# Decays between tokens from two matmuls with fixed weights instead of four float32 ones

## The chip, the cores and the metric

The kernel runs on one core of a Trainium2 chip. The metric is the device time of one execution in microseconds (us), as the median of several runs.

## The reference

Two layers of a decoder trunk on 256 tokens of width 1024. Each layer is SwiGLU, layer norm, three token mixers side by side (a gated delta rule, a sliding-window attention and a cross attention to a memory), their gated sum, layer norm, SwiGLU, layer norm. The change lies in the delta rule. There every token has a log decay g for each of four heads, and the weight with which token i acts on a later token c of the same block is the exponent of the sum of g over the tokens after i up to c:

```
g = jnp.cumsum(g, axis=-1)
tril = jnp.tril(jnp.ones((C, C), bool))
decay = jnp.exp(jnp.where(tril, g[..., :, None] - g[..., None, :], NEG_INF))
a = jnp.where(strict, jnp.einsum('bhncd,bhnsd->bhncs', k_beta, k) * decay, 0.0)
qk = jnp.where(tril, jnp.einsum('bhncd,bhnsd->bhncs', q, k) * decay, 0.0)
```

The kernel computes the same with blocks of 128 tokens in place of 64.

## The kernel before

Tokens come in two blocks of 128 (index c or tb). Weights stream from HBM in one fixed order, as units of 128x1024 float32. A unit is split on the chip: ACT casts it to fp32r (whi), DVE subtracts that from the original (wlo, L123), and every large product is three fp32r matmuls, high by high, high by low, low by high (mm3). Five buffers each for whi and wlo rotate, and the split of a unit begins when PE gives a buffer back.

The two FFN stages of a layer enclose the mixers. In the mixers PE's order is fixed by the program: the projections are generators that yield after each unit, and weave puts small steps of the mixers between the units. The other engines' orders come from a planner that goes by the order of the program and by when it expects operands; they are fixed before the run, and each engine takes its instructions in that order.

The steps around the change, in PE's order:

- the projection of the memory queries, four units with two tiles each (256 columns), with tok_v after the third;
- one unit for the keys and values of the window;
- the projection of the window queries, four units. After the first, decay (sums of g from the start of a block, 8 columns). After the second, spread(0) and x_scores(0), the latter twelve matmuls of 256 columns. After the third, spread(1). After the fourth, products(0, 0) and products(0, 1);
- the gates' units, with 512 columns, and in them x_scores(1), products(1, ...) and the inverses, which GpSimd (POOL) computes for blocks of 16.

g itself comes from a chain of some twenty small DVE operations on 128x8 (L607 to L631). GpSimd makes the product of a triangle with g for both blocks (L671, into TM[c][:, 0]). spread(c) turns that product, as the weights, into a bank of PSUM with four matmuls of 128 columns, one per head, against the other triangle (tri). DVE adds the mask dtm (L656) and ACT takes the exponent (L657). products(c, hh) multiplies keys by keys and keys by queries and DVE scales the result by the decays (L668).

Of the kernel before, what the change touches and what calls it, by code (L numbers as in the profile page):

```python
# [11 lines left out]
F32R = mybir.dt.float32r  # L12
I32 = mybir.dt.int32
AF = mybir.ActivationFunctionType
ALU = mybir.AluOpType
AX = mybir.AxisListType

P = 128
# [20 lines left out]
def tile_trunk(ctx, tc, x, xT, mem, memT_, wst, lnp, memln, cvw, rows, cst, out):  # L39
    nc = tc.nc  # L40
# [3 lines left out]
    pc = ctx.enter_context(tc.tile_pool(name="pc", bufs=1))  # L44
    praw = ctx.enter_context(tc.tile_pool(name="praw", bufs=4))
    pu = ctx.enter_context(tc.tile_pool(name="pu", bufs=1))
    p2 = ctx.enter_context(tc.tile_pool(name="p2", bufs=2))
# [7 lines left out]
    def nm(s):  # L55
        uid[0] += 1
        return f"{s}_{uid[0]}"
# [4 lines left out]
    def T(pool, shape, tag, dt=F32, bufs=None):  # L62
        pool = pn if pool is pu and tag in NEAR else pool
        kw = {} if bufs is None else {"bufs": bufs}
        return pool.tile(shape, dt, tag=tag, name=nm(tag), **kw)
# [7 lines left out]
    def sm():  # L73
        return T(psS, [P, 512], "sm")
# [7 lines left out]
    tri = cs[:, C_TRI:C_TRI + P]  # L82
    mlt = cs[:, C_LT:C_LT + P]
    dtm = cs[:, C_DTM:C_DTM + P]

    def over4(ap):
        return ap.unsqueeze(1).to_broadcast([P, 4, ap.shape[-1]])
# [34 lines left out]
    def split(hi, lo, src):  # L122
        return nc.scalar.copy(hi, src).ins, nc.vector.tensor_tensor(lo, src, hi.bitcast(F32), op=ALU.subtract).ins  # L123
# [3 lines left out]
    def pe(ins):  # L127

        return tc.keep_in_program_order(ins) if pinned[0] else ins

    def matmul(*a, **k):
        return pe(nc.tensor.matmul(*a, **k))  # L132
# [10 lines left out]
    def weave(work, steps):  # L143

        for n, _ in enumerate(work, 1):
            for f in steps.get(n, ()):
                f()

    def projB(xt, nt, kpu, behind=None):
        g = projB_parts(xt, nt, kpu, behind)  # L150
        while True:
            try:
                next(g)
            except StopIteration as e:
                return e.value

    def projB_parts(xt, nt, kpu, behind=None):
        banks = [acc().rearrange("p (t s) -> p t s", t=2) for _ in range((nt + 1) // 2)]
        for uu in range(KD // kpu):
            hi, lo = unit(behind=behind)  # L160
            for kk in range(kpu):
                k = uu * kpu + kk
                for t in range(nt):
                    c = (kk * nt + t) * P
                    o = banks[t // 2][:, t % 2, :]
                    lastt = t % 2 == 1 or t == nt - 1
                    matmul(o, hi[:, c:c + P], xt[0](k), start=(k == 0 and t % 2 == 0), stop=False, skip_group_check=True)
                    matmul(o, hi[:, c:c + P], xt[1](k), start=False, stop=False, skip_group_check=True)
                    matmul(o, lo[:, c:c + P], xt[0](k), start=False, stop=(k == KD - 1 and lastt), skip_group_check=True)
            yield  # L170
        return banks

    def halves(xt, use):

        for i in range(2):
            (b,) = yield from projB_parts(xt, 2, 4)
            use(i, b)
# [66 lines left out]
    def acc_of(t):  # L244
        return (lambda k: t[0][:, k, :], lambda k: t[1][:, k, :])
# [183 lines left out]
    def begin(nxt, hT):  # L429
        nxt.first(hT, 0)  # L430
        nxt.first(hT, 1)
        nxt.out(0, nxt.bank)
# [72 lines left out]
    def memory_kv(mT, behind):  # L505
        mx = (lambda k: mT[k // 4][:, k % 4, :], lambda k: mT[2 + k // 4][:, k % 4, :])
        mkT = (T(pu, [P, 4, S], "u10", F32R), T(pu, [P, 4, S], "u7", F32R))
        for i, b in enumerate(projB(mx, 4, 2)):
            split(*(t[:, 2 * i:2 * i + 2, :] for t in mkT), b)
        mv_ = T(pu, [P, 2, 512], "u11")  # L510
        outs = [[acc()] for _ in range(2)]
        projA(mx, 512, 2, KD, outs, behind=behind, held=range(4))
        for tb in range(2):
            nc.scalar.copy(mv_[:, tb, :], outs[tb][0])
        return mkT, mv_

    def mixers(l, hT, mkT, mv_, post):
        xt = acc_of(hT)
# [79 lines left out]
        def col(tag):  # L598
            return T(pu, sh, tag)
# [30 lines left out]
        g = col("g")  # L630
# [15 lines left out]
        TM = [T(pu, [P, 2, 4, P], f"w{2 + c}") for c in range(2)]  # L646
        AK = [T(pu, [P, 4, 2, P], f"u{12 + c}") for c in range(2)]
        hb = lambda ap: ap.unsqueeze(2).to_broadcast([P, 4, P])

        def spread(c):  # L650

            gm, dt = TM[c][:, 0], TM[c][:, 1]
            ps = sm().rearrange("p (h c) -> p h c", h=4)
            for h in range(4):
                matmul(ps[:, h, :], gm[:, h, :], tri, start=True, stop=True)
            nc.vector.tensor_tensor(dt, ps, over4(dtm), op=ALU.add)  # L656
            nc.scalar.activation(dt, dt, AF.Exp)  # L657

        def products(c, hh):
# [6 lines left out]
            for j in range(2):  # L666
                h = 2 * hh + j
                nc.vector.scalar_tensor_tensor(AK[c][:, h], TM[c][:, 1][:, h, :].unsqueeze(1).to_broadcast([P, 2, P]), cS[:, c, h:h + 1], ps[:, j], op0=ALU.mult, op1=ALU.mult)  # L668

        for c in range(2):  # L670
            nc.gpsimd.tensor_tensor(TM[c][:, 0], over4(mlt), hb(g[:, c, :]), op=ALU.mult)  # L671


        xq = (T(pu, [P, 4, S], "u4", F32R), T(pu, [P, 4, S], "u6", F32R))
# [139 lines left out]
        def use_sq(i, b):  # L814
            split(*(t[:, 2 * i:2 * i + 2, :] for t in sq_), b)

        weave(halves(xt, use_xq), {3: [tok_v]})
        (b,) = projB(xt, 1, 8)
        for kv in range(2):
            hs = slice(kv * 64, kv * 64 + 64)  # L820
            split(swk[0][hs, kv, :], swk[1][hs, kv, :], b[hs, 0, :])
        weave(halves(xt, use_sq), {
            1: [decay],
            2: [lambda: spread(0), lambda: x_scores(0)],
            3: [lambda: spread(1)],
            4: [lambda: products(0, 0), lambda: products(0, 1)]})

# [243 lines left out]
    ps = sm()  # L1071
# [7 lines left out]
    def xres(tb):  # L1079
        load(hres[tb], x[tb * P:(tb + 1) * P, :])  # L1080

    def small():
        load(rw, rows.rearrange("l r -> (l r)").partition_broadcast(P))
        load(cw, cvw)

    ends = None
    for l in range(NL):
        mT = []
        mid = memory_T(mT, l)
        if l == 0:  # L1090

            more = {4: lambda *a: xres(0), 6: lambda *a: xres(1), 8: lambda *a: small()}
        post = Post(lnp[l, 0, 0], lnp[l, 0, 1])
        f1.rest(hT, 4, [((pu, "u0"), (pu, "u1")), ((pu, "u2"), (pu, "u3"))], post, mid, ends, {} if l else more)
        kv = memory_kv(mT, post.end)
        if l == 0:
            nc.scalar.activation(nea, rw[:, :, 8:12], AF.Exp)
            nc.vector.tensor_scalar(nea, nea, -1.0, None, ALU.mult)
        post2 = Post(lnp[l, 1, 0], lnp[l, 1, 1])
        mixers(l, post.hT, *kv, post2)  # L1100
        f2 = Ffn()
        begin(f2, post2.hT)
        last = l == NL - 1
        post = Post(lnp[l, 2, 0], lnp[l, 2, 1], last)
        f2.rest(post2.hT, 6, [((pu, a), (pu, b)) for a, b in (("u0", "u1"), ("u2", "u3"), ("u4", "u5"), ("u6", "u13"))], post, behind=post2.end)
        ends = post.end
        if not last:
            f1, hT = Ffn(), post.hT
            begin(f1, hT)
# [87 lines left out]
```

## Time and profile before

| what | before |
|---|---|
| median of 3 runs | 1274.8 us (1274.46 to 1275.08) |
| the profiled execution's own time | 1274.36 us |
| its span, first to last instruction | 1272.6 us |
| PE, PE weight loads | 1260.9 us (99%), 1073.9 us (84%) |
| DVE, ACT, GpSimd | 865.0 us (68%), 660.8 us (52%), 206.9 us (16%) |
| DMA | 261.40 MB, mean 205 GB/s |

Busy times of PE are of overlapping matmuls, whose ends are modelled; what a matmul costs in a stream is read from the distance of the starts.

### The profile page before, as it was taken

Reading aid. Unit: us, or ns where it says so; the run is one execution under the profiler, and the core shown is the slowest. Engines: PE = TensorE matmul, PEld = TensorE weight load, DVE = VectorE, ACT = ScalarE, POOL = GpSimd, SP = SyncE. Lnnn points to the kernel's source line nnn. Section 1 sums busy time; section 2 is a strip of 40 time slices with the busy share of each in tenths; the row PEclk is TensorE's granted clock in tenths of the full one; section 3 lists DMA queues with packets and bytes.
Section 4 is the critical chain, followed back from the end, with each engine's and each line's share of the span. In section 5 each row is a group of like instructions: output and inputs, shape, how many; then the busy total and the mean of one; then the engine's idle time right before and its main releaser. Section 6 shows DMA issues by size and latency. Waiting matters only on the chain.

```text
span 1272.6 us, 18763 instructions
## 1 busy us (share of the span) xinstructions
PE 1260.9 (99%) x6948; PEld 1073.9 (84%) x6948; DVE 865.0 (68%) x1271; ACT 660.8 (52%) x980; POOL 206.9 (16%) x365
## 2 busy tenths in 40 slices
PE   9999999999999999999999999999999999999997
PEld 6888889999878888888888888899987788888886
DVE  5788576897657776665676665759867388666555
ACT  6556444655664544544454554456556564444541
POOL 0232100002311102221012220000024101122200
PEclk9999999999999999999999999999999999999999
DMA  8988755655534748777667877556453356577772
GB/s 296 305 274 280 254 209 164 206 166 142 171 118 138 245 135 264 240 242 221 218 208 242 255 254 215 182 184 213 152 168 133 100 185 229 172 247 244 241 231 73
DMA packets 77499, 261.40 MB, mean 205 GB/s; under 512 B 11904, under 2 KB 13056, under 8 KB 77408
## 3 DMA queue, kind: packets, MB, share of 16 engines
q1 hardware_dynamic: 66320, 232.53, 56.1%
q0 software_dynamic: 11088, 27.68, 7.8%
q8 instruction: 54, 0.88, 0.3%
q14 instruction: 37, 0.30, 0.1%
HBM read 246.40 MB, written 13.76 MB: 204 GB/s over the span
## 4 chain that ended last, share of the span: by engine, by line
PE 96%; DVE 2%; DMA 1%; ACT 1%; issue 0%; SPq 0%; DVEq 0%; ACTq 0%
PE acc L132 85%; PE at L132 4%; PE sm L132 3%; PE sm L135 2%; DVE wlo L123 1%; DMA raw<-in_wst_dram 1%; PE acc L326 1%; PE acc L327 1%; PE acc L329 1%; PE at L135 1%; ACT whi L123 1%; DVE h L289 0%; DVE pp L734 0%; DVE w L938 0%; SPq L115 0%
## 5 line engine op out<-in xcount | busy, mean ns | idle before, releaser
L123 DVE TENSOR_TENSOR wlo<-raw,whi 128x1024 fp32r<-128x1024 f32 (+2 forms) x403 | 488.8, 1220 | 284.9 <-ACT whi L123 282.8
L123 ACT CAST whi<-raw 128x1024 fp32r<-128x1024 f32 (+2 forms) x403 | 413.5, 1033 | 403.7 <-PE acc L132 322.0
L132 PE MATMUL acc<-whi,hT 128*128 128x512 f32 (+1 forms) x1824 | 562.7, 386 | 0.9 <-ACT whi L123 0.9
L132 PEld LDWEIGHTS acc<-whi,hT 128*128 128x128 f32 x1824 | 340.3, 188 | 70.1 <-ACT whi L123 2.5
L132 PE MATMUL acc<-wlo,hT 128*128 128x512 f32 (+1 forms) x912 | 350.3, 384 | 0.5 <-DVE wlo L123 0.5
L132 PE MATMUL acc<-whi,u 128*128 128x512 f32 x812 | 259.6, 392 | 0.0
L132 PEld LDWEIGHTS acc<-wlo,hT 128*128 128x128 f32 x912 | 171.4, 188 | 33.5 <-DVE wlo L123 1.2
L132 PEld LDWEIGHTS acc<-whi,u 128*128 128x128 f32 x812 | 152.3, 188 | 32.1 <-DVE u L123 0.5
L132 PE MATMUL acc<-wlo,u 128*128 128x512 f32 x406 | 158.2, 390 | 0.0
L356 POOL DMA_DIRECT2D tr<-t x176 | 96.3, 554 | 304.5 <-DVE t L350 296.4
L132 PE MATMUL acc<-hT,whi 128*128 128x256 f32 x672 | 122.2, 284 | 0.0
L132 PEld LDWEIGHTS acc<-hT,whi 128*128 128x128 f32 x672 | 104.6, 192 | 0.0
L132 PE MATMUL acc<-hT,wlo 128*128 128x256 f32 x336 | 95.0, 283 | 0.0
L132 PEld LDWEIGHTS acc<-wlo,u 128*128 128x128 f32 x406 | 76.3, 188 | 15.3
L132 PEld LDWEIGHTS acc<-hT,wlo 128*128 128x128 f32 x336 | 64.3, 192 | 0.0
L357 POOL DMA_DIRECT2D pt<-tr x44 | 25.0, 569 | 200.1 <-DMA tr<-t 129.1
L347 ACT ACTIVATE t<-acc 128x256 f32<-128x256 f32 x88 | 33.5, 380 | 37.1 <-PE acc L132 37.1
L132 PE MATMUL acc<-u,u 128*128 128x512 f32 x186 | 46.4, 394 | 0.0
L348 DVE TENSOR_TENSOR t<-t,acc 128x256 f32<-128x256 f32 x88 | 36.6, 416 | 8.6 <-ACT t L347 5.3
L993 POOL TENSOR_TENSOR u<-u,gt 128x512 f32<-128x512 f32 x16 | 20.7, 1295 | 124.9 <-DVE gt L991 124.9
L132 PEld LDWEIGHTS acc<-u,u 128*128 128x128 f32 x186 | 34.6, 188 | 7.5
L546 DVE SCALAR_TENSOR_TENSOR t<-acc,cw,t 128x255 f32<-128x255 f32 (+2 forms) x72 | 34.4, 478 | 1.0
(236 smaller groups left out, 1158.3 us busy)
## 6 DMA issues: line engine op xcount, KB each, us to landing
raw<-in_wst_dram SPq DMA_DIRECT2D x409, 512.0 KB, 4.4
tr<-t POOLq DMA_DIRECT2D x176, 64.0 KB, 3.9
pt<-tr POOLq DMA_DIRECT2D x44, 256.0 KB, 4.9
raw<-in_wst_dram SPq DMA_DIRECT2D x16, 324.0 KB, 3.0
gB<-in_lnp_dram SPq DMA_DIRECT2D x6, 512.0 KB, 5.4
bB<-in_lnp_dram SPq DMA_DIRECT2D x6, 512.0 KB, 6.2
w<-dr POOLq DMA_DIRECT2D x4, 512.0 KB, 11.0
t<-in_xT_dram SPq DMA_DIRECT2D x4, 256.0 KB, 5.4
```

The source lines that it names most:

```text
L123: return nc.scalar.copy(hi, src).ins, nc.vector.tensor_tensor(lo, src, hi.bitcast(F32), op=ALU.subtract).ins
L132: return pe(nc.tensor.matmul(*a, **k))
L135: return pe(nc.tensor.transpose(*a))
L326: nc.tensor.matmul(ps, hT[0][:, k, ts], hi[:, c], start=k == 0, stop=False)
L327: nc.tensor.matmul(ps, hT[0][:, k, ts], lo[:, c], start=False, stop=False)
L329: nc.tensor.matmul(ps, hT[1][:, k, ts], hi[:, c], start=False, stop=k == KD - 1)
L347: act = nc.scalar.activation(t[:, :, tb, :], g, AF.Silu).ins
L348: ins = nc.vector.tensor_tensor(t[:, :, tb, :], t[:, :, tb, :], u, op=ALU.mult).ins
L356: nc.gpsimd.dma_start(d[:, :, q].rearrange("b c x -> c b x"), z[32 * q:32 * q + 32].rearrange("c (b x) -> c b x", b=4))
L357: back = nc.gpsimd.dma_start(y, d.rearrange("b c q x -> (b c) (q x)")).ins
L546: nc.vector.scalar_tensor_tensor(yc[:, j, d:], b[:, j, :S - d], w[:, t:t + 1], yc[:, j, d:], op0=ALU.mult, op1=ALU.add)
L993: nc.gpsimd.tensor_tensor(mg[tb][:, js], mg[tb][:, js], gt[tb][:, js], op=ALU.add)
```

## The change

The triangle that was a weight's mask and the triangle that was streamed change places. GpSimd now multiplies tri by g. The new step spread_parts(c) splits that product into a high and a low fp32r part, in a tile of the pool p2 under the tag of the gates' tiles; the steps are placed after the first and the third unit of the memory queries. spread(c) then issues two matmuls of 512 columns, all four heads at once, with the fixed triangle `later` as weights for both: the high part and the low part, summed in the bank. `later` is an fp32r copy of mlt, made once by ACT, in the first layer.

```
+    later = pc.tile([P, P], F32R, name="later")
...
         def spread(c):
 
-            gm, dt = TM[c][:, 0], TM[c][:, 1]
+            dt = TM[c][:, 1]
             ps = sm().rearrange("p (h c) -> p h c", h=4)
-            for h in range(4):
-                matmul(ps[:, h, :], gm[:, h, :], tri, start=True, stop=True)
+
+            for n in range(2):
+                matmul(ps, later, gms[c][n], start=n == 0, stop=n == 1)
             nc.vector.tensor_tensor(dt, ps, over4(dtm), op=ALU.add)
             nc.scalar.activation(dt, dt, AF.Exp)
...
+        gms = {}
         for c in range(2):
-            nc.gpsimd.tensor_tensor(TM[c][:, 0], over4(mlt), hb(g[:, c, :]), op=ALU.mult)
+            nc.gpsimd.tensor_tensor(TM[c][:, 0], over4(tri), hb(g[:, c, :]), op=ALU.mult)
+
+        def spread_parts(c):
+            both = T(p2, [P, 2, 4, P], "gt", F32R)
+            gms[c] = both[:, 0], both[:, 1]
+            split(*gms[c], TM[c][:, 0])
...
-        weave(halves(xt, use_xq), {3: [tok_v]})
+        weave(halves(xt, use_xq), {1: [lambda: spread_parts(0)], 3: [tok_v, lambda: spread_parts(1)]})
...
         if l == 0:
+            nc.scalar.copy(later, mlt)
```

## Rows read from the trace of the kernel before

**Rows 1.** The page's engine summary: busy time, share of the span, instructions.

```profile
span 1272.6 us, 18763 instructions
PE 1260.9 (99%) x6948; PEld 1073.9 (84%) x6948; DVE 865.0 (68%) x1271; ACT 660.8 (52%) x980; POOL 206.9 (16%) x365
```

**Rows 2.** Waits of PE, whole span: total us, times, longest; first and last of five.

```profile
PE sm L1073 <- DVE pp L1070: 1.5, 1, 1.5
...
PE sm L132 <- DVE w L938: 0.3, 2, 0.2
```

**Rows 3.** Chain of waits, the spreads of both layers: start us, us, what.

```profile
284.73 0.89 PE sm L132 x8
...
289.92 0.89 PE sm L132 x8
...
914.24 0.89 PE sm L132 x8
...
919.43 0.89 PE sm L132 x8
```

**Rows 4.** View of the tile sm, spread's matmuls: duration ns min/median/max, first and last start.

```profile
L132 PE MATMUL sm<-cs,w x32: 270/275/275, 284.6 to 920.0; 128*128 128x128 f32 x32
```

**Rows 5.** Timeline of PE, first layer: start us, us, operation, count.

```profile
284.57 1.05 PE L132 MATMUL sm<-cs,w 128*128 128x128 f32 x8
285.38 1.66 PE L132 MATMUL at<-u,u 128*128 128x256 f32 x12
286.88 0.40 PE L132 MATMUL acc<-hT,whi 128*128 128x256 f32 x2
...
289.76 1.05 PE L132 MATMUL sm<-cs,w 128*128 128x128 f32 x8
...
293.53 0.39 PE L132 MATMUL sm<-u 128*128 128x128 f32 x2
```

**Rows 6.** Timeline of PE, second layer, the first units of the gates.

```profile
925.28 0.63 PE L132 MATMUL acc<-whi,hT 128*128 128x512 f32 x2
925.75 0.39 PE L132 MATMUL acc<-wlo,hT 128*128 128x512 f32 x1
925.97 0.63 PE L132 MATMUL acc<-whi,hT 128*128 128x512 f32 x2
...
927.59 1.57 PE L132 MATMUL at<-u,u 128*128 128x256 f32 x12
929.00 0.38 PE L132 MATMUL sm<-u 128*128 128x128 f32 x2
```

**Rows 7.** View of the tile u: splits of 128x512 read from SBUF.

```profile
L123 ACT CAST u<-pt x44: 611/612/622, 41.8 to 1221.7; 128x512 fp32r<-128x512 f32 x44
L123 DVE TENSOR_TENSOR u<-pt,u x44: 646/650/693, 43.9 to 1223.0; 128x512 fp32r<-128x512 f32 x44
```

**Rows 8.** Timeline of POOL, first layer; in brackets idle time before and its releaser.

```profile
279.52 3.02 POOL L671 TENSOR_TENSOR w<-cs,g 128x512 f32<-128x512 f32 x2 [48.68 <-DVE g L631]
```

**Rows 9.** Timeline of DVE, first layer.

```profile
279.27 0.17 DVE L631 TENSOR_TENSOR g<-spp,nea 128x8 f32<-128x8 f32 x1
279.53 2.11 DVE L123 TENSOR_TENSOR wlo<-raw,whi 128x1024 fp32r<-128x1024 f32 x1
...
283.48 1.23 DVE L123 TENSOR_TENSOR wlo<-raw,whi 128x1024 fp32r<-128x1024 f32 x1 [0.64 <-ACT whi L123]
...
284.81 0.69 DVE L644 TENSOR_TENSOR u<-u,ks 128x512 f32<-128x512 f32 x1
285.66 0.69 DVE L656 TENSOR_TENSOR w<-sm,cs 128x512 f32<-128x512 f32 x1 [0.16 <-PE sm L132]
```

**Rows 10.** Timeline of ACT, first layer.

```profile
278.45 1.05 ACT L123 CAST whi<-raw 128x1024 fp32r<-128x1024 f32 x1 [1.35 <-PE acc L132]
...
282.01 0.37 ACT L123 CAST swk<-acc 64x256 fp32r<-64x256 f32 x1 [2.25 <-DVE swk L123]
...
283.47 0.18 ACT L640 ACTIVATE eg<-sm 128x16 f32<-128x16 f32 x1
```

## Prediction, made before the changed kernel was built

> **What bounds the kernel now.** I read the views from coarse to fine. The engine summary comes first: TensorE (PE) is busy for 1260.9 of the 1272.6 us between the first and the last instruction, VectorE (DVE) for 68% and ScalarE (ACT) for 52% [rows 1]. Next the list of waits for PE: five groups stand in it, from 1.5 us down to 0.3 us, and with the three between them (0.9, 0.5, 0.4) they come to 3.6 us over the whole kernel [rows 2]. PE waits for almost nothing, so time taken from its stream should be time taken from the kernel, and work added to DVE or ACT is free until it makes PE wait. The chain of waits says the same for the place of the change: in it the eight records of one call of spread stand as a piece of PE work of their own, 0.89 us long, twice in each layer and so four times in all [rows 3]. No wait stands between these pieces and their neighbours.
>
> **The removed matmuls.** Each spread issues four float32 matmuls of 128 columns. The trace has each of them as two records: 32 records for 2 layers, 2 token blocks and 4 heads [rows 4]. From the start of the first record at 284.57 to that of the next matmul at 285.38 is 0.81 us, so 0.10 us a record [rows 5]. The durations of 270 to 275 ns say nothing of this, since records overlap; starts are what to compare. There is a second, smaller part. The twelve score matmuls that follow this spread take 1.50 us from their first start to the start of what follows (285.38 to 286.88) [rows 5]; the same twelve in the next stage, which follow fp32r matmuls, take 1.41 us (927.59 to 929.00) [rows 6]. So going from float32 back to fp32r costs about 0.08 us, and that goes too. Together a spread costs 0.89 us, the figure of the chain.
>
> **The added matmuls.** Two fp32r matmuls of 512 columns, with `later` as weights, once with the high and once with the low part of the masked decays. The gate stage has matmuls of exactly that kind (128x128 weights, 512 columns, fp32r): three of them run from 925.28 to 925.97, 0.23 us each [rows 6]. Two are 0.46 us. As bounds for the pair I take 0.45 us (the score matmuls of 256 columns run at 1.41 / 12 = 0.118 us, so 256 more columns cost 0.113, and 1024 columns without any fixed part four times that) and 0.54 us (0.46 and one more change of 0.08 us, if going from 256 to 512 columns costs what the change of type does). The value 0.46 is from rows of the same operation, so I take it.
>
> The PE sum: 0.89 - 0.46 = 0.43 us for a spread, four spreads, 1.7 us; with the bounds 1.4 to 1.8 us.
>
> **The added splits.** spread_parts puts one ACT copy and one DVE subtraction of 128x512 from SBUF on those engines for each block. The same pair with SBUF input is in the trace as the split of the turned FFN tiles: 612 ns on ACT, 650 ns on DVE [rows 7]. Four of each add 2.4 us to ACT and 2.6 us to DVE over the kernel. The question is whether the first low part is there when PE comes to it, as PE's order is fixed in this stage and a late operand stops all that is behind it. The path in the first layer (the second repeats it 629.5 us later, by the pieces of the chain [rows 3]): g is done at 279.44 [rows 9]; the two GpSimd products run from 279.52 to 282.54, 1.51 us each, so that of block 0 ends at 281.03 [rows 8]. ACT then has nothing to do until 282.01 [rows 10], so the copy may end at 281.64. DVE comes free of its weight split at 281.64, and is idle for 0.64 us of the time before 283.48 [rows 9]. That weight split took 2.11 us where its neighbour at 283.48 took 1.23 us, and it ran beside the GpSimd products. With the same stretch, 650 ns becomes 1.1 us, and the low part is ready near 282.8. PE wants the high part at 284.57 and the low part 0.23 us later, at 284.80. The margin is 2.0 us. For block 1 the inputs come 1.5 us later and PE wants them 5.2 us later, so that one has more.
>
> The Trainium skill bears on that stretch: "SBUF — State Buffer", section "Who interferes with whom", says that the only contention is for the port pair that DVE shares with GpSimd, and that it is an exclusive lock, held for a whole instruction. By it the low part of block 0 could not begin before the second product ends at 282.54, and would end at 283.2: a margin of 1.6 us in place of 2.0. The row of 2.11 us agrees only in part, as a subtraction that had waited out the first product to 281.03 could not have been done before 282.2 and was done at 281.64. Either way the sum stays, and only the stall below comes a little nearer.
>
> What is queued behind the added work: on ACT and DVE these are the weight splits. ACT's cast at 278.45 began when PE gave up a buffer [rows 10]; five buffers rotate, so what is cast there is used some four units later, and a unit is 2.9 us of PE work (286.88 to 289.76) [rows 5]. A delay of a microsecond or two is covered by that; without cover each late microsecond would be one on PE. The masked sum at 285.66 [rows 9] may come up to 1.3 us later (two subtractions), less what PE is earlier; it must free its PSUM bank before the first products at 293.53 [rows 5], which leaves over 6 us. GpSimd does the same two products with another mask, nothing in them changes. The `later` tile is one ACT copy of 128x128 in the whole kernel, traced ahead of the mixers of the first layer and wanted at 284.57; its price lies between the 0.18 us of an exponent of 128x16 and the 0.37 us of a cast of 64x256 [rows 10], and on PE it is nothing. No DMA is added and no queue of SP or GpSimd is passed.
>
> **The sum.** The profiled execution took 1274.36 us, of which 1272.6 are the span; less 1.7 us it is 1272.6. It lies 0.4 us under the median of the three runs, 1274.8; on the median's footing I say 1273.1 us, by the price bounds 1273.0 to 1273.4. What the medians of two kernels can be told apart by is about 0.2% here, 2.5 us, so the likely outcome, 0.13% faster, counts as no change.
>
> **The rivals.**
>
> *A late low part (slower).* Engines take their instructions in the order in which they were put. If DVE's order has the low part of block 0 behind the weight split at 283.48 and the scaling at 284.81, which ends at 285.5 [rows 9], it is done near 286.1, and PE stands still from 284.80 for 1.3 us. In both layers that is 2.6 us, against a gain of 1.7: 1275.7 us, on the other side of before. It decides from 285.7 on, when the stall of a layer passes its gain of 0.86 us. For it speaks that DVE has only short gaps there; against it that the split is ready three microseconds before it is needed and stands early in the program, ahead of that scaling. 8 in 100. To be slower by over 0.2% it would need more than 2.1 us of stall in a layer; with other shifts of the engines' orders that I can't price, I give 4 in 100.
>
> *The gain is given back.* PE is earlier by 0.86 us in a layer, but a later stage waits for something that did not move, such as the GpSimd chain that makes the 16x16 inverses. Then the time is before's, 1274.8. Against it: that chain starts from the products, which move with PE, and PE's waits in all are 3.6 us [rows 2]. 12 in 100.
>
> *More than the sum.* The engines' orders shift, and some of the 3.6 us of PE's waits go as well. With half of them, 1273.1 - 1.8 = 1271.3. It needs luck rather than a cause: 12 in 100.
>
> *The pair costs as much as the eight did.* If an fp32r matmul with this operand ran at the float32 price per column, two of 512 would take 0.81 us and only the 0.08 us of the change of type would be left: 1274.5. The gate stage has the same operand types at 0.23 us: 3 in 100.
>
> **How the numbers follow.** The forecast, 1273.1 us, has 61 in 100; the rivals 8, 4, 12, 12 and 3. The range of 1271.3 to 1275.0 holds the forecast, the gain given back, the equal price and the upper half of the lucky case, and leaves out the late low part, the unpriced slower case and the rest of the lucky one. Faster by over 0.2% means under 1272.3: the lucky case and a few in 100 of the forecast, 0.16. Slower by over 0.2% means above 1277.3: 0.04. The rest, 0.80, is no change to be told.
>
> **What would show it.** In the new trace the piece of spread in the chain should be about 0.46 us, two records with starts 0.23 us apart, and the next fp32r matmul should follow without the 0.08 us. Over the kernel 32 records of 128 columns go and 8 of 512 come. PE should show no new wait on a DVE or ACT instruction that writes the new split tile. If PE waits there, the late low part holds; if the pieces are short and the time does not move, the gain was given back, and the list of PE's waits would name where. A time above 1275 or below 1271.5 would mean that the engines' orders decide, and not the price of the matmuls.

## The result, and the profile after

The changed kernel takes 1277.45 us (median of 21 runs), the kernel before 1275.25 us (21 runs beside them): a ratio of 1.0021, 95% interval 1.0012 to 1.0031. The forecast was 1273.1 us, no change that can be told, and its range ended at 1275.0. The kernel became slower, by 2.2 us. The mean granted clock of PE is recorded for each of the 21 executions: the twelve at 0.998 or 0.999 have a median of 1276.8 us, 1.6 above before's, and the nine at 0.997 or less one of 1279.2.

The profiled execution of after took 1278.84 us. In its summary PE is as full as before [rows 1], but the span is 4.4 us longer:

```profile
span 1277.0 us, 18721 instructions
PE 1262.5 (99%) x6924; PEld 1074.2 (84%) x6924; DVE 868.8 (68%) x1275; ACT 662.9 (52%) x985; POOL 206.6 (16%) x365
```

**The matmuls do what was forecast.** The chain of waits of after (start us, us, what) has the four spreads at 0.46 us instead of 0.89 [rows 3]:

```profile
285.23 0.46 PE sm L133 x2
289.98 0.46 PE sm L133 x2
915.26 0.46 PE sm L133 x2
920.01 0.46 PE sm L133 x2
```

PE's timeline (start us, us, operation, count; in brackets the idle time before it and what ended it) shows the pair 0.46 us before the twelve score matmuls, these 1.41 us before what follows [rows 5, 6], and no wait for a low part:

```profile
281.75 0.51 PE L133 MATMUL sm<-g,cs 128*128 128x8 f32 x4
285.07 0.62 PE L133 MATMUL sm<-gt,later 128*128 128x512 f32 x2
285.53 1.58 PE L133 MATMUL at<-u,u 128*128 128x256 f32 x12
286.94 0.40 PE L133 MATMUL acc<-hT,whi 128*128 128x256 f32 x2
...
344.01 1.08 PE L133 MATMUL at<-pt,swv 128*64 128x512 f32 x4 [1.05 <-DVE pp L742]
...
974.54 1.08 PE L133 MATMUL at<-pt,swv 128*64 128x512 f32 x4 [1.54 <-DVE pp L742]
```

**The gain ends at the window attention's values.** These are the matmuls `at<-pt,swv`, 60 us behind the spreads. PE now waits for them in both layers, where it used to wait 0.18 us. The same place is at the head of PE's waits (us in total, times, longest), where it stood with 0.4 us before:

```profile
PE at L133 <- DVE pp L742: 2.6, 2, 1.5
...
```

I measure each layer from the first matmul of the decays (`sm<-g,cs`), which lies ahead of everything the change touches. Before, the values start 62.27 us behind it; here are the two rows of PE's timeline of before:

```profile
281.25 0.51 PE L132 MATMUL sm<-g,cs 128*128 128x8 f32 x4
...
343.52 1.08 PE L132 MATMUL at<-pt,swv 128*64 128x512 f32 x4 [0.18 <-DVE pp L734]
```

After, it is 62.26 us in the first layer (344.01 - 281.75) and 62.76 in the second. So the 0.86 us by which PE should be ahead at this place are gone, and in the second layer 0.5 us more.

**And the clock falls behind the second wait.** The table by stretch (from:to, length, busy us of PE, PEld, DVE, ACT and POOL, granted clock, DMA share, GB/s) has PE at its lower level (0.50, that is 1.2 of 2.4 GHz) for over 6 us behind the stop of 1.54 us:

```profile
970.00:974.50 4.50, 3.00 (x14) 2.09 (x12) 4.50 (x6) 1.10 (x2) 0.00 (x0) 1.00 0.54 179
974.50:977.00 2.50, 2.46 (x60) 1.65 (x62) 2.46 (x3) 1.50 (x3) 0.00 (x0) 0.83 0.91 316
977.00:979.00 2.00, 2.00 (x19) 1.65 (x16) 1.38 (x5) 1.02 (x5) 0.00 (x0) 0.50 0.89 303
979.00:981.00 2.00, 2.00 (x6) 1.56 (x5) 0.00 (x0) 0.54 (x3) 0.00 (x0) 0.50 0.59 211
981.00:983.00 2.00, 2.00 (x6) 1.57 (x5) 0.00 (x0) 0.00 (x0) 0.00 (x0) 0.51 0.02 6
983.00:985.00 2.00, 2.00 (x10) 1.61 (x10) 1.25 (x2) 1.97 (x5) 0.00 (x0) 1.00 0.00 0
```

Laid beside before, PE's stream is 2.9 us later at the end of that stretch than at its start. That is most of this execution's 4.4 us; the other pieces (+0.5 ahead of the first spreads, -0.9 at the spreads of each layer, +0.9 and +1.4 at the values, +0.5 between the layers) come to 1.5 us together.

**What PE waits for** is read on DVE, in the order of its queue. The last instruction of the GpSimd chain of 16x16 inverses (`inverses`) releases a transpose on DVE (`begin_inverse`); behind it stand four weight splits, then the mask additions of the window scores, which give PE the bank for the values. DVE's timeline of before:

```profile
302.71 1.25 DVE L668 SCALAR_TENSOR_TENSOR u<-w,cS,sm 128x256 f32<-128x256 f32 x3
...
336.23 0.45 DVE L895 STREAM_TRANSPOSE w<-w 128x256 f32<-128x256 f32 x1 [2.40 <-POOL w L802]
338.24 4.63 DVE L123 TENSOR_TENSOR wlo<-raw,whi 128x1024 fp32r<-128x1024 f32 x4 [1.57 <-ACT whi L123]
342.79 1.28 DVE L734 SCALAR_TENSOR_TENSOR pp<-at,cs 128x512 f32<-128x512 f32 x2
```

and of after:

```profile
303.85 1.25 DVE L670 SCALAR_TENSOR_TENSOR u<-w,cS,sm 128x256 f32<-128x256 f32 x3
...
338.40 0.45 DVE L903 STREAM_TRANSPOSE w<-w 128x256 f32<-128x256 f32 x1 [4.94 <-POOL w L810]
338.77 4.59 DVE L124 TENSOR_TENSOR wlo<-raw,whi 128x1024 fp32r<-128x1024 f32 x4
343.28 1.28 DVE L742 SCALAR_TENSOR_TENSOR pp<-at,cs 128x512 f32<-128x512 f32 x2
```

Before, DVE stands 1.57 us behind the transpose for ACT: the chain of inverses had that much room in the first layer. After, the transpose is 2.17 us later by the clock of the span and 1.67 later behind the decays, nothing is left between it and the splits, and from the transpose to the values it is 5.61 us in both layers (338.40 to 344.01, 968.93 to 974.54). In the second layer the transpose is only 0.73 us later behind the decays (57.15 us against 56.42), but there before had no such room: its weight splits followed the transpose at once (967.74 us, behind 967.18 + 0.45). The chain of inverses now sets PE's time in both layers.

Two things make it later against the decays. The scaling of the products on DVE, which feeds it, ends 23.35 us behind the decays (303.85 + 1.25 - 281.75) instead of 22.71. And the transfer that spreads the products' diagonal blocks over the partitions (`w<-dr`, 2 x 512 KB, from its issue on GpSimd to the first instruction that reads it) is longer. POOL's timeline of before, first layer:

```profile
311.61 1.24 POOL L788 DMA_DIRECT2D w<-dr  x2 [3.24 <-DMA dr<-t]
321.85 0.40 POOL L800 TENSOR_TENSOR t<-w,t 128x120 f32<-128x120 f32 x1 [9.01 <-issue]
```

The same of after:

```profile
312.87 1.24 POOL L796 DMA_DIRECT2D w<-dr  x2 [3.37 <-ACT u L124]
324.04 0.40 POOL L808 TENSOR_TENSOR t<-w,t 128x120 f32<-128x120 f32 x1 [9.94 <-issue]
```

10.24 us before, 11.17 after (second layer 11.66 and 12.02). So the transfer is issued 0.76 and 0.61 us later behind the decays, in the first and the second layer, and takes 0.93 and 0.36 us longer. Each of its two issues takes GpSimd 0.62 us in both kernels, so it is not the issuing that became longer. SP's timeline has the weight load nearest to it, of before:

```profile
312.92 0.33 SPq L115 DMA_DIRECT2D raw<-in_wst_dram  x1
```

and of after:

```profile
312.53 0.33 SPq L116 DMA_DIRECT2D raw<-in_wst_dram  x1
```

Before, SP issues it 1.31 us behind the transfer; after, 0.34 us ahead, as PE frees its buffer about 0.9 us earlier and the transfer is issued 0.76 us later. In the second layer after's transfer stands in the chain of waits as one piece:

```profile
942.73 11.88 DMA w<-dr
```

### The profile page after: what moved, and what is told of

Read it like the earlier page. It is cut to its first block, busy times and chain, and to the rows that moved or that the text cites. A ratio compares the mean times of both kernels' runs of the same rounds, so it can differ in the third digit from the quotient of the medians.

```text
span 1277.0 us, 18721 instructions
## 1 busy us (share of the span) xinstructions
PE 1262.5 (99%) x6924; PEld 1074.2 (84%) x6924; DVE 868.8 (68%) x1275; ACT 662.9 (52%) x985; POOL 206.6 (16%) x365
## 4 chain that ended last, share of the span: by engine, by line
PE 92%; DVE 3%; DMA 2%; POOL 1%; issue 1%; ACT 1%; SPq 0%; DVEq 0%; ACTq 0%; POOLq 0%
PE acc L133 81%; PE at L133 3%; PE sm L133 3%; DMA raw<-in_wst_dram 2%; PE sm L136 2%; DVE wlo L124 1%; DMA w<-dr 1%; PE acc L330 1%; PE acc L327 1%; PE acc L328 1%; PE at L136 1%; ACT whi L124 1%; POOL t L809 0%; POOL t L808 0%; DVE h L290 0%
```

## The experiments

The theory after this reading was that the splits cost more than the matmuls gain, as they delay the scaling and with it the start of the chain. Its rival: the chain was just short enough before, and whatever makes PE earlier, or the chain later, ends in the same wait. "Lag" is the time from the decays to the end of the scaling, "values' waits" are PE's waits in the first and the second layer; before has a lag of 22.71 us and waits of 0.18 and 0.18. Each ratio is against runs of before on the same chip. Where a kernel has unread work, or leaves some out, it is said.

**The splits without the matmuls.** Before, with the two splits of each layer (a cast and a subtraction for each block) written to tiles that nothing reads: unread work.

```
+        def spread_parts(c):
+            both = T(p2, [P, 2, 4, P], "gt", F32R)
+            gms[c] = both[:, 0], both[:, 1]
+            split(*gms[c], TM[c][:, 0])
...
-        weave(halves(xt, use_xq), {3: [tok_v]})
+        weave(halves(xt, use_xq), {1: [lambda: spread_parts(0)], 3: [tok_v, lambda: spread_parts(1)]})
```

> The kernel before, with spread's float32 matmuls as they were, and only the splits of the masked decays added (a copy on ACT and a subtraction on DVE for each block; nothing reads them). PE's work is that of before. Theory 1, DVE's queue: the two subtractions in each layer (2.35 us in the changed kernel's trace) make DVE's queue late, so the scaling of the products, GpSimd's inverses and the transpose that waits for them are late too, and PE waits at the first values of the window attention. Then the transpose should start about 1.5 to 2 us later than in before, PE should wait there 0.5 us in the first layer and 0.7 to 1.5 us in the second, and the time should be 1276.5 to 1277.5. Theory 2, PE early: the changed kernel only brings PE to that wait earlier while the GpSimd chain stays where it was. Then nothing changes here: 1275.25, with waits of 0.2 us.

1279.53 us, ratio 1.0024 (1.0013 to 1.0035); lag 23.34, values' waits 1.52 and 2.47, and the clock fell behind the second. So the splits alone, with the old matmuls, make the kernel slower.

**The changed kernel without DVE's share.** Here the low part is left out: a tile of zeros is multiplied in its place, so the decays are those of the rounded high part.

```
-                matmul(ps, later, gms[c][n], start=n == 0, stop=n == 1)
+                matmul(ps, later, (gms[c][0], over4(none))[n], start=n == 0, stop=n == 1)
...
-            split(*gms[c], TM[c][:, 0])
+            nc.scalar.copy(gms[c][0], TM[c][:, 0])
```

> The changed kernel without the low part: the second matmul of 512 columns reads a tile of zeros that is made once, and DVE gets no subtraction. The decays are those of the rounded high part alone. PE's work is that of the changed kernel. Theory 1, DVE's queue: the waits at the first values of the window attention stay at before's 0.2 us, the GpSimd chain moves with PE, and the 1.7 us of the matmuls stay: 1273.5. Theory 2, PE early: the chain stays and PE meets it 0.4 us earlier in the first layer and 0.9 us earlier in the second: waits of 0.6 and 1.0 us, the gain is gone: 1275.

1279.92 us, 1.0032 (1.0018 to 1.0047); lag 23.4, waits 1.52 and 1.52. DVE's subtractions were not needed for the delay; the theory that blamed them alone fell.

**The low part on GpSimd** in place of DVE.

```
-            split(*gms[c], TM[c][:, 0])
+            nc.scalar.copy(gms[c][0], TM[c][:, 0])
+            nc.gpsimd.tensor_tensor(gms[c][1], TM[c][:, 0], gms[c][0].bitcast(F32), op=ALU.subtract)
```

> The changed kernel with the low parts subtracted by GpSimd in place of DVE. GpSimd has nothing else to do there; at 1.3 to 1.5 us each, after both products, the low part of block 0 is ready near 283.9 on the scale of before's first layer, and PE wants it at 284.8, so PE should not wait there. Theory 1, DVE's queue: as without the low part, 1273.5, and faster than both kernels. Theory 2, PE early: 1275, with waits of 0.6 and 1.0 us at the first values of the window attention.

1276.8 us, 1.0008 (0.9997 to 1.0019), which can't be told from before; lag 23.53, waits 2.59 and 1.54, a fall of the clock in the first layer of the profiled execution.

**ACT's casts alone**, and **DVE's subtractions alone** (before, with unread work of the one engine or the other).

```
+            nc.scalar.copy(gms[c][0], TM[c][:, 0])
```

> The kernel before, with only the two copies of the masked decays to fp32r added on ACT in each layer (nothing reads them, no subtraction on DVE, PE as in before). ACT takes them in order and waits for GpSimd's second product before the next weight cast, which then starts 1.2 us later. If ACT's queue by itself makes the scaling of the products late, by way of the weight casts that DVE waits for and the exponents of the memory scores, the time from decay to the end of the scaling is 23.4 us as in the kernel without the low part (before: 22.71). If only DVE's subtractions do it, it is 22.7.

```
+            nc.vector.tensor_tensor(gms[c][1], TM[c][:, 0], TM[c][:, 0], op=ALU.subtract)
```

> The kernel before, with DVE's two subtractions of 128x512 per layer alone (from the masked product to itself, into tiles that nothing reads) and without ACT's casts: unread work. The run with ACT's casts alone had the scaling of the products end 0.7 us later after the decay's start on PE than before (23.42 against 22.71 us in the first layer). If ACT's casts are the whole delay: here that distance stays at 22.6 to 22.9 us, PE's waits at the window attention's values stay under 0.3 us, and the time is 1274.5 to 1276.0 us. If DVE's subtractions delay the chain as much by themselves: 23.2 us or more and waits of 1 us or more.

Lag 23.41 and 23.28 us with the casts, 23.21 with the subtractions; one run each, 1277.6 and 1276.9 us. Either half delays the scaling by 0.5 to 0.7 us, and both together by no more than 0.65. My guess of 22.6 to 22.9 for the subtractions failed. The first half is seen on ACT in after: a cast waits 1.36 us for GpSimd's second product, and the weight split and the exponent of the decays stand behind it. The exponent comes 2.80 us behind the decays (284.55 - 281.75), where before it was 2.22 (283.47 - 281.25) [rows 10]. ACT's timeline of after:

```profile
281.09 0.62 ACT L124 CAST gt<-w 128x512 fp32r<-128x512 f32 x1 [0.83 <-POOL w L674]
283.07 0.62 ACT L124 CAST gt<-w 128x512 fp32r<-128x512 f32 x1 [1.36 <-POOL w L674]
283.60 1.04 ACT L124 CAST whi<-raw 128x1024 fp32r<-128x1024 f32 x1
284.55 0.18 ACT L641 ACTIVATE eg<-sm 128x16 f32<-128x16 f32 x1
```

**The chain late by itself.** Before, with four idle copies of 0.29 us on GpSimd ahead of the chain's first transfer; nothing else moves.

```
+            spare = T(p2, [P, 2, 4, 16], "t2", bufs=4)
+            nc.gpsimd.tensor_copy(spare, cp)
+            nc.gpsimd.tensor_copy(cp, spare)
+            nc.gpsimd.tensor_copy(spare, cp)
+            nc.gpsimd.tensor_copy(cp, spare)
```

> The kernel before with four idle copies of 128x128 (0.29 us each) on GpSimd ahead of the transfer that starts its inverses, so that the chain of the inverses is some 1.2 us late and nothing else changes. If that chain sets when PE may go on, as theory 1 has it, the second layer, where before's DVE goes straight from the transpose into its weight splits, shows a wait of about 1.4 us in place of 0.2, and the first layer, where DVE had waited 1.57 us for ACT after the transpose, shows 0.2 to 0.4 us: about 1276.5, more if the clock falls. If the chain has slack, 1275.25.

1279.33 us, 1.0026 (1.0014 to 1.0038); lag 22.71 as before, yet waits of 1.76 and 1.52. The chain was made later than meant: one of the copies took 1.17 us, and the transfer `w<-dr` was issued 3.0 and 2.7 us later than before, where I had expected 1.2. So a late chain of inverses is enough for the same wait and a loss as large, but this run does not say how late it must be.

The splits alone, the two kernels without DVE's subtraction and this one all took longer than the times expected of them. Part of that is the clock, as the last expectation allowed for: the mean granted clock was 0.997 or less in 8 of 11 executions of the splits alone, 6 of 7 without the low part, 6 of 12 with it on GpSimd and 8 of 12 with the late chain, against 2 of 29 of before. The other executions of these kernels have medians of 1276.4, 1277.3 (one execution), 1275.5 and 1276.7 us.

**The chain's transpose out of the way.** On DVE the transpose is put behind the mask additions that PE waits for (`wpr["mask"]` is their last instruction), once in before and once in after.

```
-            with tc.issue_after(wpr["end"]):
+            with tc.issue_after(wpr["mask"]):
...
-            3: [lambda: w_turn(0, 1), begin_inverse],
-            4: [lambda: w_scores(1, 0)]})
+            3: [lambda: w_turn(0, 1)],
+            4: [lambda: w_scores(1, 0), begin_inverse]})
```

> The kernel before with one thing moved: DVE's transpose that waits for GpSimd's inverses stands in DVE's order behind the masked scores of the second token block and not ahead of the four weight splits before them. So the values of the window attention need no longer wait for the inverses. If that transpose holds PE in the changed kernel (theory 1), it also holds before a little (0.2 us in each layer, more in executions where the transfer for the inverses is long), and this kernel is 0.4 to 1 us faster than before, 1274.5, with a smaller spread of its times. If the wait only moves to the doubling steps that need the transpose, 1275.3.

> The changed kernel with the transpose moved in the same way. Theory 1: with PE no longer held there, the matmuls' gain stays: no wait at the first values of the window attention, and 1.7 us less than the kernel before with the same move, 1272.8 to 1273.5. If the gain of the matmuls is not real, or is lost in some other way, it takes as long as the kernel before with the move, or as long as the changed kernel, 1277.

Before with it: 1275.37 us, 0.9997 (0.9988 to 1.0005). After with it: 1274.78 us, 0.9989 (0.9980 to 0.9997), waits 0.26 and 0.67. Where the transpose can't hold PE, the changed kernel is the faster one, and moving the transpose does nothing for the kernel before. The two differ by 0.6 us, though, of the 1.7 that the matmuls give: the changed kernel's time is above what I had expected. DVE's timeline of after with the transpose moved, first layer:

```profile
338.01 4.71 DVE L124 TENSOR_TENSOR wlo<-raw,whi 128x1024 fp32r<-128x1024 f32 x4 [4.42 <-ACT whi L124]
342.64 1.27 DVE L742 SCALAR_TENSOR_TENSOR pp<-at,cs 128x512 f32<-128x512 f32 x2
343.84 0.43 DVE L903 STREAM_TRANSPOSE w<-w 128x256 f32<-128x256 f32 x1
```

**No large splits at all.** After, with the 128x8 logarithms split first, and GpSimd masking both parts; then with the transpose moved as well.

```
+        gp = [T(pu, sh, f"g{n}", F32R) for n in range(2)]
+        split(*gp, g)
...
-            split(*gms[c], TM[c][:, 0])
+            for n in range(2):
+                nc.gpsimd.tensor_tensor(both[:, n], over4(tri), hb(gp[n].bitcast(F32)[:, c, :]), op=ALU.mult)
```

> The changed kernel, but g itself (128x8) is split into a high and a low part, and GpSimd masks both; the triangle holds only 0 and 1, so the masked parts are the same numbers. The splits of 128x512 on ACT and DVE are gone, GpSimd has four products in place of two. Theory 1, now for the queues of both ACT and DVE: the end of the scaling of the products comes about 22.7 us after decay, less the 0.9 us that PE is earlier, as against 23.35 in the changed kernel; PE's wait at the values of the window attention is under 0.5 us, and the time is 1274 to 1275. If what holds DVE up is not the work in the queues but its running beside GpSimd, the scaling is as late as in the changed kernel or later, since GpSimd is busy for 6 us there and not 3: 1277.

> Both: g split ahead of the masks, and the transpose moved behind the masked scores. Theory 1: neither the queues nor the chain of the inverses holds PE: 1272.8 to 1273.3, faster than both kernels by what the matmuls gave, and the least spread of times of all. If a third wait takes over, its place is to be read from PE's waits.

1277.63 us, 1.0016 (1.0006 to 1.0026), lag 22.99, waits 1.09 and 1.10; with the transpose moved 1274.39 us, 0.9987 (0.9978 to 0.9996). More than half of the extra lag is gone, but not the waits: both times are above what theory 1 had, and with the transpose moved PE still waits 0.74 us in each layer.

**The mask additions at a high priority**, in before, in after and in the version above.

```
+                with tc.high_priority(offset=2 * AHEAD):
```

> The kernel before, with the masked scores of the window attention given a higher priority in the plan, so that DVE does the two of the second token block after the transpose and two weight splits, where it did them after four. The values then follow the transpose by some 3.4 us at the least, where it was 5.6. Theory 1: the wait of 0.2 us at these values goes, and so do the longer ones of executions in which the inverses are late: 1274.7, with a smaller spread. The transpose stays where it is, so the doubling steps do not get it later.

> The changed kernel with the same priority. Theory 1: 2.2 us of slack at the values is more than the 0.9 to 1.5 us that PE waited there, so that wait goes, the matmuls' gain of 1.7 us stays, and this takes 1.5 to 1.7 us less than the kernel before with the same priority: 1273.1. If the gain is lost in another place as well, the difference is smaller, and PE's waits name the place.

> The same priority, with g split ahead of the masks (no splits of 128x512 on ACT and DVE, four products on GpSimd). The chain of the inverses is about 0.4 us earlier than in the kernel with the priority alone (22.7 to 23.0 us from decay to the end of the scaling, against 23.4). Theory 1: as that one or a little faster, 1272.9 to 1273.1, with fewer late executions.

1279.41, 1278.92 and 1279.86 us, all slower (1.0037, 1.0027, 1.0034). The priority changed ACT's order too, and a wait on ACT came up at the doubling steps of the inverse; in after with it:

```profile
PE sm L133 <- ACT w L863: 2.8, 2, 1.4
```

These three tell nothing of the question but that the wait at the values can be removed at the price of another.

**Block 1's split held back** until ACT has the decays' exponent, so that ACT doesn't stand before GpSimd's second product; then with the transpose moved as well.

```
+        def late_parts():
+            with tc.issue_after(gms["eg"]):
+                spread_parts(1)
...
-            1: [decay],
+            1: [decay, late_parts],
```

> The changed kernel with the split of block 1 held until the decay's exponent on ACT is issued, so that ACT doesn't stand before GpSimd's second product. The same work, another order. If what delays the scaling is ACT's standing for GpSimd: the distance from the decay's start to the scaling's end falls from 23.4 to 22.7 to 23.0 us, PE's waits at the window attention's values fall from 1.05 and 1.54 us to 0.8 to 1.2, the clock doesn't fall, and the time is 1274.5 to 1276.3 us, under the changed kernel's 1277.5. If it is the mere count of work on ACT and DVE: 23.3 us or more, and 1277 to 1278 us.

> The same, and also the transpose that opens the inverse's sequel placed behind the window attention's mask additions on DVE, as in the run that put the changed kernel under the kernel before. By the theory no chain is left that stops PE (waits at the values under 0.5 us) and the 1.7 us of the matmuls come through: 1273.3 to 1274.3 us, 0.3 to 0.8 under the changed kernel with the transpose moved alone (1274.8) at most. If another chain is next, 1274.5 to 1275.5.

The lag is back at before's (22.72, and 22.71 in the second layer), but 1277.43 us, 1.0021 (1.0012 to 1.0031), and waits of 1.99 and 1.50: the theory that the scaling's delay is the loss fell here. The transfer is issued as long behind the decays as before (30.51 and 30.34 us against 30.36 and 30.34), but takes 13.55 and 13.33 us against 10.24 and 11.66, with the nearest load 0.27 and 0.44 us behind it instead of 1.31 and 1.32. POOL's timeline of this kernel, first layer:

```profile
313.89 1.24 POOL L800 DMA_DIRECT2D w<-dr  x2 [3.40 <-ACT gt L987]
327.44 0.40 POOL L812 TENSOR_TENSOR t<-w,t 128x120 f32<-128x120 f32 x1 [12.31 <-issue]
```

With the transpose moved: 1274.13 us, 0.9995 (0.9986 to 1.0003).

**The transfer and the weight loads.** By now there were two transfers from each of 17 traces. Sorted by when SP issued the weight load nearest to the transfer's issue:

| weight load nearest to the transfer | kernels | transfers | us |
|---|---|---|---|
| 1.2 us or more behind it | before, and its versions with the transpose moved or the masks first | 6 | 10.24 to 11.88, mean 11.05 |
| from 1.7 us ahead to 0.75 us behind | all others | 28 | 10.42 to 14.32, median 12.4 |

The groups overlap: eleven of the 28 took no longer than the longest of the six. They also differ in more than the load: in every kernel of the second group the scaling or the chain is later, or PE earlier, or both. To test the load, a one-element write by GpSimd into the load's buffer, placed behind the transfer's issue, holds the load. Three kernels: after with the hold and block 1's split held back, after with the hold alone, and all with the transpose moved.

```
+                if clear:
+                    with tc.issue_after(clear):
+                        nc.gpsimd.memset(raw[0:1, 0:1], 0.0)
                 nc.sync.dma_start(raw[:, c], src[:, c])
...
-            us = [unit() for _ in range(4)]
+            us = [unit(clear=gms["moved"] if k == 3 and n == 0 else None) for k in range(4)]
```

> The changed kernel with block 1's split held back (as in the run before), and one more thing: the weight load that SP issues beside the 1 MB transfer of the products' blocks is held until that transfer has been issued (a GpSimd write of one element into the load's buffer, placed behind the transfer's issue). In the traces so far the transfer took 10.2 to 11.9 us (six of six) where that load came 1.2 us or more behind it, as in the kernel before, and 10.4 to 14.3 us (28) where it came between 1.7 us ahead and 0.75 us behind, as in the changed kernel. If the collision is what keeps the chain late: transfers of 10.2 to 11.9 us, PE's waits at the window attention's values at 0.2 to 0.9 us, 1274.0 to 1275.3 us. If the transfer's length has nothing to do with the load: 12 to 14 us still, waits of 1 to 2 us, 1276 to 1278 us as without the hold.

> The changed kernel with that hold alone. The scaling of the products is still 0.65 us late, so if the collision is the other half: transfers of 10.2 to 11.9 us, waits of 0.2 to 1.3 us, the clock mostly kept, 1274.5 to 1276.0 us. If not: as the changed kernel, waits of 1 to 1.6 us and 1276.5 to 1278 us.

> All three together: block 1's split held back, the load held back, and the transpose behind the mask additions. If the transpose alone already takes the chain off PE's path, the other two give nothing more: 1274.0 to 1274.4, as late_parts_turn (1274.1). If the later steps of the inverse were still bound by the chain: 1273.0 to 1273.9.

1273.2 us (0.9981, interval 0.9972 to 0.9990), 1273.58 us (0.9986, 0.9977 to 0.9995) and 1272.87 us (0.9979, 0.9970 to 0.9989), all faster than before (1275.48 us beside them). The hold cleared more than I meant: it caught the load 2.6 us ahead of the transfer, and with it the next, so none lies between 4.3 us ahead and 1.32 behind. The transfers took 8.34 to 9.62 us in all six cases, shorter than before's and than I had expected, and the times lie under the expected ones. Moving the transpose as well adds 0.3 us at most. POOL's timeline of after with the hold alone, first layer:

```profile
312.84 1.23 POOL L799 DMA_DIRECT2D w<-dr  x2 [3.21 <-ACT u L127]
314.04 0.09 POOL L118 MEMSET raw<- 1x1 f32 x1
321.81 0.40 POOL L811 TENSOR_TENSOR t<-w,t 128x120 f32<-128x120 f32 x1 [7.68 <-DMA w<-dr]
```

The two loads behind it, on SP's:

```profile
314.16 0.80 SPq L119 DMA_DIRECT2D raw<-in_wst_dram  x2
```

And PE's:

```profile
281.80 0.51 PE L136 MATMUL sm<-g,cs 128*128 128x8 f32 x4
...
343.19 1.08 PE L136 MATMUL at<-pt,swv 128*64 128x512 f32 x4 [0.18 <-DVE pp L745]
```

The transfer takes 8.97 us, PE waits 0.18 us, and the values start 61.39 us behind the decays: 0.88 us less than before's 62.27, where the prediction's two spreads gave 0.86. The lag of this kernel is still 23.45 us. The table by stretch shows the two microseconds from the transfer's issue (DMA share and GB/s at the end of each row), in after with the hold:

```profile
312.84:314.84 2.00, 2.00 (x12) 1.64 (x11) 0.50 (x1) 0.07 (x1) 1.29 (x3) 1.00 0.23 45
```

in after, and in before:

```profile
312.87:314.87 2.00, 2.00 (x13) 1.64 (x12) 0.43 (x1) 0.14 (x1) 1.23 (x2) 1.00 0.76 238
311.61:313.61 2.00, 2.00 (x14) 1.75 (x13) 1.84 (x2) 1.11 (x3) 1.23 (x2) 1.00 0.59 205
```

The DMA engines are a quarter busy at that time with the hold, and three quarters without it. In before they are 0.59 busy, so the hold does more than put before's state back. The kernel before with the hold was not run; its waits of 0.18 us at the values are already those of the kernels with the hold. The Trainium skill has a rule that fits ("DMA: Bandwidth & Descriptors", section "Queues, rings and completion order"): each DMA engine takes turns between the queues that have work for it, packet by packet. That the transfer is shortest where the loads are held agrees; the order of packets itself no run here shows.

## Why the prediction was wrong

**The matmul sum was right.** 0.46 us a spread in all four pieces, and 0.88 us for a layer in the kernel where nothing else stops PE, against 0.86. With the hold alone the time is 1273.58 us, with the hold and block 1's split held back 1273.2; the forecast was 1273.1. The price of the matmuls is what the working said; what it missed is what lies between them and the end.

**The low part was in time.** The rival of the late low part did not come: PE waits for no `gt`, the tile of the split. The estimate of 282.8 us for the first low part was too early, though. DVE's timeline of after has the subtraction, beside GpSimd's second product:

```profile
282.06 1.52 DVE L124 TENSOR_TENSOR gt<-w,gt 128x512 fp32r<-128x512 f32 x1
```

It ended at 283.6, 1.7 us before PE wants it (285.07 + 0.23). Of the two readings in the prediction the one by the Trainium skill ("SBUF — State Buffer", "Who interferes with whom": the port pair is held for a whole instruction) gave a margin of 1.6 us, mine 2.0; the row is nearer to the skill's. One reading of mine was wrong: the two GpSimd products do not take 1.51 us each, which is the mean of a merged row. POOL's timeline of before has them one by one:

```profile
279.52 1.04 POOL L671 TENSOR_TENSOR w<-cs,g 128x512 f32<-128x512 f32 x1 [48.68 <-DVE g L631]
280.52 2.02 POOL L671 TENSOR_TENSOR w<-cs,g 128x512 f32<-128x512 f32 x1
```

The first ended at 280.56, so a weight split that waited for it and then took its 1.23 us would be done at 281.79; it was done at 281.64. With that the row of 2.11 us, which the prediction found to agree only in part, agrees with the lock to 0.15 us.

**The step that failed is the one on what is queued behind the added work.** It named the weight splits and the masked sum, priced both by their consumers on PE, and called a delay of a microsecond or two covered. For block 1 it asked only whether PE gets that part in time, and not what stands behind ACT's wait of 1.36 us for GpSimd's second product. The scaling of the products hangs on the same queues of ACT and DVE, and its consumer is not PE but GpSimd, whose chain takes 32 to 34 us from there to the transpose, before and after. The scaling was 0.5 to 0.7 us later with either half of the splits.

**The rival "the gain is given back" was dismissed for a wrong reason.** It named this very chain, and I set it aside as "that chain starts from the products, which move with PE". It was not true even of its start, which came 0.76 and 0.61 us later behind the decays. The middle of the chain is a transfer that shares the DMA engines with weight loads, and those do move with PE: SP issues them when a buffer comes free. With PE 0.86 us earlier and the scaling later, the load came before the transfer instead of behind it. So the chain did not move with PE: it started later and its transfer took longer. And the room that it had could have been read in the trace of before: from the transpose to the values it took 7.29 us in the first layer (336.23 to 343.52) and 5.85 in the second, of which 5.61 are work, so it had 1.7 and 0.2 us. PE's waits [rows 2] tell only what is late now, not how much room the rest has.

**The loss beyond that gain** is the wait growing past 0.86 us, and the clock. Giving the gain back alone would have been before's time, 1275.25 us beside these runs; the executions that kept the clock lie 1.6 us above that, and the median of all 2.2. The clock entered no step of the prediction.

What is shown, then: the loss is in the chain of inverses. A late chain alone makes it, and with a chain that holds PE less, by the transpose, the hold or both, five of six versions of the changed kernel are faster than before and the sixth can't be told from it.

What made the chain late is shown only in part. The later scaling is not needed: with the lag at before's value the transfer alone kept the chain late (13.55 and 13.33 us). The hold brings the matmuls' gain back with the lag unchanged, but it shortens the transfer by 2.2 and 3.6 us against after, more than the 1.67 and 0.73 us by which after's transpose was late. So it shows that a shorter transfer is enough, and not that the load at its side was the whole of after's delay: in after's own profile the later issue (0.76 and 0.61 us) and the longer transfer (0.93 and 0.36) share it. Open is also why the transfers of the second group vary from 10.4 to 14.3 us at much the same distance of the load, and why the clock fell in some executions and not in others.

## What to carry to other kernels

When PE is at 99%, time taken from it is worth its price only as far as the nearest other chain has room; look for the engine whose queue stands idle just before PE's next hand-over, and read that idle time as the room, before the sum is made. An engine that becomes earlier also frees its buffers earlier, so list the loads that this triggers and what they then meet on the DMA engines. And when a long chain with a transfer in it is close to the path, one load held back may be worth more than the arithmetic that was saved: here it took the changed kernel from 1277.45 to 1273.58 us, where the matmuls save 1.7.

## What the hardware showed unasked

The same 1 MB transfer took 8.34 to 9.62 us with no weight load issued from 4.3 us ahead of it to 1.3 us behind, 10.24 to 11.88 with one weight load some 2 us ahead and one 1.2 us or more behind, and 10.42 to 14.32 with a load from 1.7 us ahead of its issue to 0.75 us behind.

PE's clock fell to 1.2 GHz behind some stops and not behind others of the same length: in the second layer behind 1.54 us in after, but not behind 1.54 us with the low part on GpSimd; in the kernel without the low part behind the second of two stops of 1.52 us (granted clock 0.55 from 977 to 979 us) and not behind the first (1.00 from 345 to 349 us). It fell behind 1.76, 2.47 and 2.59 us in other experiments, but not behind 1.99 us with block 1's split held back. The stop's length alone does not tell it. The kernel without the low part, behind its second stop:

```profile
977.00:979.00 2.00, 2.00 (x38) 1.74 (x33) 1.97 (x5) 0.64 (x3) 0.00 (x0) 0.55 0.87 344
```
